# Moving the load of X's second slice from ScalarE's DMA queue to SP's, behind the first slice of G

## The chip, the core and the metric

The kernel runs on one core of one Trainium2 chip. The metric is the device time in microseconds (us) of one launch. Before the change it is 163.57 us, the median of three runs (163.35 to 163.69). The profiled execution has a span of 161.9 us from its first to its last instruction; all moments below are counted from the start of that span.

## What is computed

```python
def setup_inputs():
    batch, m, k, n = 16, 512, 1024, 768
    input:       float32 [16, 512, 1024]
    grad_output: float32 [16, 512, 768]

def reference(input, grad_output):
    return np.einsum('bmk,bmn->kn', input, grad_output)   # float32 [1024, 768]
```

It is one matrix product, X^T G, with X of 8192 x 1024 and G of 8192 x 768; the sum runs over all 8192 rows. The inputs are float32 in HBM; the kernel multiplies in bf16 and adds up in float32.

## The kernel before

**Tiling.** The 8192 rows are cut into 64 slices of 128 rows, one row to a partition. A slice is X of 128 x 1024 and G of 128 x 768. The output is cut into four quarters: A and B are the upper 512 rows (left and right 384 columns), C and D the lower 512 rows (left and right). A quarter has four strips of 128 rows; one strip of one quarter for one slice is one matmul, 128 x 128 weights of X against 128 x 384 of G, into one of the eight PSUM banks. So a slice taken plainly costs 16 matmuls, in four visits of four.

**Pairs.** The string `LOADS` (L12) says how the 32 pairs of slices are taken: "s" as two plain slices, "P" as one pair that is multiplied by a scheme with seven products of half-size blocks in place of eight. The sums of blocks that it needs are made by VectorE (DVE) ahead of time (L125 to L154), and its products m, n, o, p, q, A and D are added up in `macc` and `acc`. The first seven pairs (slices 0 to 13) and the last two are plain.

**Order.** The order of the work on TensorE (PE), VectorE, ScalarE (ACT) and GpSimd (POOL) is written out by hand: `manual_schedule` (L77) keeps each engine's instructions as the program gives them. `ORDER` (L16) is the list of visits. In "C2:4!0,0,0,0" the letter is the quarter or product, 2 the slice up to which it is carried, 4 how many of its strips ScalarE evicts from PSUM (VectorE does the others), and "!" that the banks are evicted after the visit. The first visits are A1 (slice 0, quarter A, four matmuls; its first strip is evicted by VectorE, the other three by ScalarE), D1 (slice 0, quarter D), C2 (slices 0 and 1, quarter C: eight matmuls, for each strip slice 0 and then slice 1), B2, D3, A2, B4 and so on. The first matmul on slice 1 is thus the second one of C2, the tenth of the real work.

**How the data come.** There are three ways in, all in front of the loop over `ORDER`:

- SP's queue loads G of slice 0 as float32 into `gf`, the left half at L81 and the right half at L83.
- ScalarE's queue loads X of slice 0 into `xf[0]` (L82) and, behind it, X of slice 1 into `xf[1]` (L84), both float32.
- POOL's queue loads everything else, G of slice 1 first (L111), then X and G of slices 2 and 3 (L113, L111), then whole pairs (L106, L107). These transfers turn float32 into bf16 on the way. They are issued in the order of use, as early as buffers come free; 14 pair buffers of each kind (`PAIRS_HELD`) stand for them, two of the X buffers being `xf`.

**Rounding.** What came as float32 is rounded to bf16 by `round_by` (L206), in pieces, partly on VectorE and partly on ScalarE. For slice 0: the left half of G and the whole of X ahead of the first visit (L209 to L215). The right half of G is rounded by VectorE between A1 and D1 (L360), so on VectorE it stands behind the eviction of A1's first strip (L301). X of slice 1 is rounded just ahead of C2:

```python
            round_by("DVE", x1, xf[1], 4 * P, 6 * P)
            round_by("ACT", x1, xf[1], 6 * P, 8 * P)
            round_by("DVE", x1, xf[1], 0, 2 * P)
            round_by("ACT", x1, xf[1], 2 * P, 4 * P)
```

C2 reads columns 4P to 8P of it, B2 the others. While the first transfers run, twelve matmuls on constants (L89) keep TensorE busy.

Of the kernel before, what the change touches and what calls it, by code (L numbers as in the profile page):

```python
# [9 lines left out]
P = 128  # L10
# [32 lines left out]
def kernel(  # L43
# [6 lines left out]
    nc = tc.nc  # L50
# [10 lines left out]
    X = input.rearrange("b m k -> (b m) k")  # L61
# [17 lines left out]
    xf = [pairs.tile([P, K], f32, name=f"xf{s}", tag="xp") for s in range(2)]  # L79
# [1 line left out]
    nc.sync.dma_start(out=gf[:, 0:NH], in_=G[0:P, 0:NH])  # L81
    nc.scalar.dma_start(out=xf[0], in_=X[0:P, :])  # L82
    nc.sync.dma_start(out=gf[:, NH:N], in_=G[0:P, NH:N])  # L83
    nc.scalar.dma_start(out=xf[1], in_=X[P : 2 * P, :])  # L84

    ones = nc.const_aps.tensor(1.0, (P, P), bf16)
    wps = psum.tile([P, 512], f32, name="bank7")
# [313 lines left out]
```

## Time and profile before

| what | value |
|---|---|
| time | 163.57 us (163.35 to 163.69) |
| span of the profiled execution | 161.9 us, granted clock 1.000 |
| TensorE busy | 157.1 us, 97% |
| VectorE, ScalarE, POOL busy | 139.6, 94.6, 34.6 us |
| read from HBM, written to it | 58.72 MB, 3.15 MB |
| first real matmul, end of A1 | 5.21 us, 6.17 us |
| start of D1 | 7.12 us |
| end of the last matmul | 158.42 us |

The page's first part gives busy time by engine, its second the span in 40 slices, and its fourth the chain of work that ended last. The rate of the DMA engines is counted by the bytes that they write. The transfers that turn float32 into bf16 write half of what they read, so that a stretch with only these shows half of the rate at which HBM is read. The timeline gives start, length, engine, line and tile of instructions, with the idle time ahead of them and what ended it in square brackets. For a transfer, the view of a tile gives the time from its issue to its landing.

### The profile page before, as it was taken

The page shows a single profiled execution, that of the slowest core. Times are in us where ns is not written, and L with a number is a line of the kernel's source. Part 1 is how long each engine was busy: PE and PEld are TensorE (multiplying, and loading weights), DVE is VectorE, ACT ScalarE, POOL GpSimd, SP SyncE. Part 2 cuts the span into 40 slices and gives each one's busy share as a digit, 9 for nine tenths or more (in the row PEclk, how much of TensorE's full clock was granted, in tenths as well). Part 3 has the DMA queues.
Part 4 walks back from the last instruction along what each step waited for, and adds up shares of the span by engine and source line. Part 5 has one row for each costly group of instructions (what it writes and reads, how often), then busy time and mean ns, then how long its engine had stood idle before and what let it go on. Part 6 is the DMA issues. An engine that isn't in the chain of part 4 may idle for free.

```text
span 161.9 us, 2755 instructions
## 1 busy us (share of the span) xinstructions
PE 157.1 (97%) x951; PEld 92.7 (57%) x951; DVE 139.6 (86%) x289; ACT 94.6 (58%) x221; POOL 34.6 (21%) x69
## 2 busy tenths in 40 slices
PE   8799999999999999999999999999999999999992
PEld 2365666566565565655656666666555666666661
DVE  0557947469979999999989999999998999999992
ACT  3766004745587799359749684661446646888410
POOL 7442222122221212222212222222212100000000
PEclk9999999999999999999999999999999999999999
DMA  5999999999999999999999999999999999902675
GB/s 171 294 213 211 211 216 215 211 211 215 214 213 212 212 213 213 213 211 215 212 213 213 212 216 214 220 207 212 211 211 214 212 214 214 187 5 97 225 283 173
DMA packets 12397, 33.40 MB, mean 206 GB/s; under 512 B 1376, under 2 KB 4192, under 8 KB 12384
## 3 DMA queue, kind: packets, MB, share of 16 engines
q0 software_dynamic: 9360, 28.64, 89.4%
q1 hardware_dynamic: 2592, 3.47, 6.2%
q10 hardware_dynamic: 432, 1.11, 1.8%
q8 instruction: 7, 0.11, 0.3%
q14 instruction: 6, 0.05, 0.1%
HBM read 58.72 MB, written 3.15 MB: 382 GB/s over the span
## 4 chain that ended last, share of the span: by engine, by line
PE 93%; DMA 3%; DVE 1%; SPq 0%; issue 0%
PE bank L285 93%; DMA gf<-in_grad_output_dram 3%; PE bank L336 0%; DVE acc L344 0%; SPq L81 0%; DVE gp L206 0%
## 5 line engine op out<-in xcount | busy, mean ns | idle before, releaser
L285 PEld LDWEIGHTS <-xp 128*128 128x128 bf16 x649 | 63.3, 98 | 43.6 <-issue 1.5
L285 PE MATMUL bank<-gp,xp 128*128 128x384 bf16 x468 | 80.9, 326 | 1.0 <-DVE gp L206 1.0
L299 ACT COPY macc<-bank 128x384 f32<-128x384 f32 x73 | 31.5, 493 | 25.0 <-PE bank L285 24.9
L303 DVE TENSOR_TENSOR acc<-bank,acc 128x384 f32<-128x384 f32 x69 | 34.7, 551 | 8.7 <-PE bank L285 8.3
L285 PEld LDWEIGHTS <-xe 128*128 128x128 bf16 x276 | 26.6, 98 | 18.5 <-DVE xe L145 0.8
L285 PE MATMUL bank<-ge,xp 128*128 128x384 bf16 x181 | 33.6, 326 | 0.0
L285 PE MATMUL bank<-gp,xe 128*128 128x384 bf16 x184 | 32.4, 326 | 0.0
L266 ACT COPY bank<-macc 128x384 f32<-128x384 f32 x56 | 25.3, 503 | 8.0 <-DVE macc L303 6.9
L299 ACT COPY acc<-bank 128x384 f32<-128x384 f32 x44 | 19.5, 486 | 15.4 <-PE bank L285 15.3
L107 POOL DMA_DIRECT2D xp<-in_input_dram x30 | 15.9, 530 | 53.1 <-DMA xp<-in_input_dram 29.8
L106 POOL DMA_DIRECT2D gp<-in_grad_output_dram x30 | 15.9, 531 | 37.5 <-DMA gp<-in_grad_output_dram 14.8
L303 DVE TENSOR_TENSOR macc<-bank,macc 128x384 f32<-128x384 f32 x44 | 22.5, 552 | 1.5 <-PE bank L285 1.2
L266 ACT COPY bank<-acc 128x384 f32<-128x384 f32 x34 | 15.2, 492 | 8.6 <-DVE acc L303 8.5
L285 PE MATMUL bank<-ge,xe 128*128 128x384 bf16 x92 | 16.6, 326 | 0.0
L145 DVE TENSOR_TENSOR xe<-xp 128x1024 bf16<-128x1024 bf16 x23 | 15.7, 684 | 0.5 <-DMA xp<-in_input_dram 0.5
L154 DVE TENSOR_TENSOR xp<-xp 128x1024 bf16<-128x1024 bf16 x23 | 15.7, 684 | 0.0
L189 DVE TENSOR_TENSOR acc<-acc,macc 128x768 f32<-128x768 f32 (+1 forms) x20 | 14.6, 791 | 0.0
L131 DVE TENSOR_TENSOR ge<-gp 128x768 bf16<-128x768 bf16 x23 | 12.7, 551 | 0.2 <-DMA gp<-in_grad_output_dram 0.2
L140 DVE TENSOR_TENSOR gp<-gp 128x768 bf16<-128x768 bf16 x23 | 12.7, 551 | 0.0
L149 DVE TENSOR_TENSOR xe<-xp 128x512 bf16<-128x512 bf16 x23 | 9.6, 418 | 0.0
L135 DVE TENSOR_TENSOR ge<-gp 128x384 bf16<-128x384 bf16 x23 | 8.1, 351 | 0.0
L89 PE MATMUL bank<-const-bfloat16-1.0 128*128 128x512 bf16 (+1 forms) x12 | 4.6, 574 | 0.8 <-PEq L385 0.8
(20 smaller groups left out, 21.4 us busy)
## 6 DMA issues: line engine op xcount, KB each, us to landing
xp<-in_input_dram POOLq DMA_DIRECT2D x30, 512.0 KB, 16.7
gp<-in_grad_output_dram POOLq DMA_DIRECT2D x30, 384.0 KB, 16.7
out_dram<-acc SPq DMA_DIRECT2D x15, 192.0 KB, 1.9
xf<-in_input_dram ACTq DMA_DIRECT2D x2, 512.0 KB, 5.0
gp<-in_grad_output_dram POOLq DMA_DIRECT2D x3, 192.0 KB, 6.6
xp<-in_input_dram POOLq DMA_DIRECT2D x2, 256.0 KB, 7.9
gf<-in_grad_output_dram SPq DMA_DIRECT2D x2, 192.0 KB, 4.6
out_dram<-acc SPq DMA_DIRECT2D x1, 128.0 KB, 1.7
```

Of the source, the lines that this page charges most:

```text
L106: nc.gpsimd.dma_start(out=gp, in_=G[rows, :].rearrange("(p m) n -> p m n", m=2))
L107: nc.gpsimd.dma_start(out=xp, in_=X[rows, :].rearrange("(p m) k -> p m k", m=2))
L131: nc.vector.tensor_add(out=ge[:, 0:2, :], in0=g[:, :, 0, :], in1=g[:, :, 1, :])
L140: nc.vector.tensor_sub(out=g[:, 1:3, :], in0=g[:, 1:3, :], in1=g[:, 3::-3, :])
L145: nc.vector.tensor_add(out=xe[:, 0:2, :].rearrange("p a k -> p (a k)"), in0=xp[:, 0, :], in1=xp[:, 1, :])
L149: nc.vector.tensor_add(out=extra[i][0][:, 2, :], in0=xp[:, 0, 0:KH], in1=xp[:, 1, KH:K])
L154: nc.vector.tensor_sub(out=x[:, 1:3, :], in0=x[:, 1:3, :], in1=x[:, 0::3, :])
L189: op(out=dst, in0=dst, in1=src)
L266: nc.scalar.copy(out=bank, in_=sum_of(p, q))
L285: nc.tensor.matmul(bank, stat, mov, start=opening and j == 0 and not carried, stop=close and j == len(items_now) - 1, skip_group_check=car ...
L299: nc.scalar.copy(out=dst, in_=bank)
L303: nc.vector.tensor_add(out=dst, in0=bank, in1=dst)
```

## The change

One line is different: the load of X of slice 1 is issued by SP rather than by ScalarE.

```diff
     nc.sync.dma_start(out=gf[:, 0:NH], in_=G[0:P, 0:NH])
     nc.scalar.dma_start(out=xf[0], in_=X[0:P, :])
     nc.sync.dma_start(out=gf[:, NH:N], in_=G[0:P, NH:N])
-    nc.scalar.dma_start(out=xf[1], in_=X[P : 2 * P, :])
+    nc.sync.dma_start(out=xf[1], in_=X[P : 2 * P, :])
```

Before, the right half of G of slice 0 (on SP's queue) and X of slice 1 (on ScalarE's) are under way at the same time. With the change they stand in one queue, G ahead of X, which is the order in which D1 and C2 use them. Nothing else differs: ScalarE has one instruction less, SP one more, ahead of the stores of the output that it issues at the end; the instructions of TensorE, VectorE and POOL stand as before.

## The prediction

> **What bounds the kernel now.** I read the page's chain of work that ended last first, then the same chain in order of time.
>
> ```profile
> PE 93%; DMA 3%; DVE 1%; SPq 0%; issue 0%
> ...
> 1.17 5.52 DMA gf<-in_grad_output_dram
> 6.69 0.02 issue
> 6.71 0.37 DVE gp L206
> 7.08 0.04 issue
> 7.12 150.51 PE bank L285 x921
> ```
>
> The end is set by one transfer, the right half of G of slice 0 (landed at 6.69), its rounding on VectorE, and then TensorE without a break to 157.6. So whatever moves D1's start at 7.12, or makes TensorE wait later, shows in the time. The waits of the first 16 us and the timeline of VectorE say how much is lost there:
>
> ```profile
> PE bank L285 <- DVE gp L206: 1.0, 1, 1.0
> ...
> 4.85 0.56 DVE L206 CAST xp<-xf 128x128 bf16<-128x128 f32 x3
> 5.72 0.56 DVE L301 COPY acc<-bank 128x384 f32<-128x384 f32 x1 [0.30 <-PE bank L285]
> 6.71 0.36 DVE L206 CAST gp<-gf 128x384 bf16<-128x384 f32 x1 [0.43 <-DMA gf<-in_grad_output_dram]
> 7.11 0.50 DVE L206 CAST xp<-xf 128x256 bf16<-128x256 f32 x2
> ```
>
> TensorE idles 0.96 us ahead of D1. VectorE is free for the rounding from 6.28 (5.72 + 0.56), so only 0.43 us of that can be won by an earlier landing. The last row is X of slice 1, landed at 1.17 + 5.9 = 7.07.
>
> Does a lead won at 7.12 last to the end? Weight loads are where TensorE's waits on data show. All their waits on a transfer, and where it is in their timeline:
>
> ```profile
> PEld L285 <- DMA xp<-in_input_dram: 0.3, 1, 0.3
> ...
> 43.93 0.44 PEld L285 LDWEIGHTS <-xp 128*128 128x128 bf16 x4 [0.28 <-DMA xp<-in_input_dram]
> ```
>
> This is X of the second "P" pair, issued at 26.02, landed 17.9 us later. Matmuls start 0.163 us apart; at this one the step is 0.226 us, a wait of 0.06 us. Up to 43.9 us the kernel is thus held by the stream of loads as well: TensorE arrives there 0.06 us early. A lead won at 7.12 ends in this wait, unless POOL's stream moves too; a lag over 0.06 us goes to the end whole.
>
> So I need the stream. Rates from the view by stretches (last column GB/s, by bytes written):
>
> ```profile
> 3.75:4.00 0.25, 0.25 (x2) 0.12 (x1) 0.00 (x0) 0.00 (x0) 0.25 (x2) 1.00 1.10 445
> 4.00:4.25 0.25, 0.25 (x2) 0.10 (x1) 0.00 (x0) 0.00 (x0) 0.25 (x2) 1.00 0.87 328
> ...
> 5.00:5.25 0.25, 0.25 (x4) 0.22 (x2) 0.25 (x3) 0.25 (x2) 0.25 (x2) 1.00 1.01 397
> 5.25:5.50 0.25, 0.25 (x3) 0.12 (x2) 0.17 (x1) 0.25 (x2) 0.25 (x1) 1.00 1.07 369
> 5.50:5.75 0.25, 0.25 (x3) 0.17 (x2) 0.03 (x1) 0.06 (x1) 0.10 (x1) 1.00 1.11 348
> 5.75:6.00 0.25, 0.25 (x3) 0.13 (x2) 0.25 (x1) 0.12 (x1) 0.00 (x0) 1.00 0.96 272
> ...
> 6.75:7.00 0.25, 0.00 (x0) 0.00 (x0) 0.25 (x1) 0.25 (x1) 0.00 (x0) 1.00 1.13 197
> ```
>
> The engines are busy throughout. A rate near 400 means float32 loads of SP and ScalarE; near 200 means POOL's, which write half of what they read. So POOL's loads, issued from 1.23 on, move nothing before about 5.3.
>
> The packet records of the trace (queue, start, duration and size of each packet) say why. A transfer of 128 rows is eight rows on each of 16 engines. A row of a half of G takes 65 ns, a row of X 159 ns, a row of POOL's G 134 ns, and an engine takes the queues with work in turn. Three facts matter:
> - SP's G ends on the 16 engines one by one, most from 5.17 to 5.63. The records don't name the engine, but for 11 of the 16 ends a row of POOL's starts 0.159 to 0.163 us later, which is one row of X, and POOL's first row is at 5.33. So POOL gets no turn on an engine while SP's and ScalarE's queues both have work there.
> - Between two transfers of one queue an engine pauses that queue for about 0.3 us (SP's left half ends at 3.71 to 4.14 on the engines, the right half begins 0.3 us later; ScalarE's at 4.03 to 4.46 likewise).
> - In ScalarE's pause SP has the engine alone, and so moves over half of the right half.
>
> **What the skill says.** The Trainium skill, "DMA: Bandwidth & Descriptors", section "Issuing engines are not separate DMA queues", says that transfers from all issuers share the same 16 engines and interleave, and that more issuers save only issue time. The trace agrees on the sharing (rates stay near 400 whoever moves). The same page, "Queues, rings and completion order", says that an engine goes round the queue rows it has work for. The trace shows this for SP with ScalarE and for ScalarE with POOL, but not for the three together. For the order within a queue I rely on the trace's records above.
>
> **The change part by part.**
> - ScalarE loses one issue (0.46 us at 1.17), SP gains one. ScalarE's next work waits for data until 4.52, and SP issues nothing else before the stores: zero.
> - X of slice 0 and the left half of G are untouched up to their ends at about 4.1. A1 stays at 5.21.
> - From 4.1 on ScalarE's queue is empty. The question is who takes its place. By the first fact above, POOL: one of the two queues that kept it out has drained. Then on an average engine the right half of G alternates with POOL: 8 x (65 + 134) = 1.6 us, against 0.3 us alone (4.6 rows) and 3.4 x (65 + 159) = 0.76, together 1.06, before. It lands 0.5 us later: 7.2 in place of 6.69; D1 starts at 7.6.
> - X of slice 1 then starts at 4.1 + 1.6 + 0.3 = 6.0 and needs 8 x (159 + 134) = 2.34 us, so ends at about 8.3. Before, it ended at 6.20 to 6.74, about 6.5, and landed at 7.07. So it lands 1.8 us later, at about 8.9.
> - Waiting behind it: on VectorE the piece for C2 (0.29 us), on ScalarE the piece for C2's last two strips (0.40 us), and behind TensorE's tenth matmul the whole rest. That matmul can start at 8.87 + 0.04 + 0.29 + 0.05 = 9.25. Before, it stood at 7.12 + 5 x 0.163 = 7.94. Lag: 1.3 us. The other pieces of X are done by 9.8 and needed from 9.9, so add nothing.
> - POOL's stream is no slower: what X of slice 1 gives up, POOL gets. G of slice 1 (before: landed at 1.23 + 6.3 = 7.53) comes over 1 us earlier, but isn't what C2 waits for.
> - The lag hides the 0.06 us wait at 43.9. Sum: +1.3 - 0.06 = +1.25, 164.8 us.
>
> For X's landing, which the trace doesn't show in this queue, the bounds are: alone on the engines from the start, 4.1 + 0.52 + 0.3 + 1.27 = 6.2 (landing about 6.8); sharing with POOL throughout, 8.3 (landing 8.9), half a us more if one slow engine lags as it does for the right half of G (most engines done by 5.6, the last at 6.34). I take 8.9: POOL's rows were waiting, and alternate one to one with ScalarE's as soon as SP is done.
>
> **The rivals.**
> - *SP goes ahead of POOL until its queue is empty.* The trace would look the same before, since it never shows POOL beside SP. Then the right half of G lands before 6.28, D1 starts at 6.28 + 0.36 + 0.04 = 6.7, X of slice 1 lands at 6.8, in time. But POOL begins at 6.2 on an average engine, where before it began at 5.45 and had done 0.5 us of work by 6.5, as if begun alone at 6.0; and in SP's pause of 0.3 us nothing moves. POOL's stream is 0.2 to 0.3 us late, and so is the load at 43.9, which eats the lead: 163.8 us. For it: POOL starts exactly when SP is done. Against it: there is no reason why SP should shut POOL out where ScalarE doesn't.
> - *Nothing to be measured.* X of slice 1 has a slack: landing at 7.07 + 0.04 + 0.29 + 0.05 = 7.45 against 7.94, so 0.5 us. If sharing costs no more than that and POOL's stream is unmoved, TensorE is at 43.9 as before: 163.5 us.
> - *Faster.* D1 starts at 6.7 (a lead of 0.43), and POOL's stream comes earlier by as much, for instance because one pause less is exposed (the rate falls to 328 in one quarter of a us at a change of transfers): 163.1 us. Against it: the engines are busy throughout before, so there is hardly idle DMA time to win, and the bytes ahead of the load at 43.9 are the same.
>
> **How the numbers follow.** POOL shares with SP: 0.62, 164.8 us. SP first: 0.22, 163.8. Nothing: 0.08, 163.5. Faster: 0.08, 163.1. The bound of 0.2% is 0.33 us. The first case is slower; the second, at +0.2 to +0.3, is mostly within and is counted as 0.04 slower and 0.18 same. So faster 0.08, same 0.26, slower 0.66. The range from 163.6 to 165.3 holds the first two cases with a late engine's 0.5 us above; it leaves out the other two.
>
> **What would show it.** If right: the rates fall below 350 from about 4.3 on rather than from 5.5; the right half of G lands near 7.2, X of slice 1 near 8.9, G of slice 1 over 1 us earlier than 7.53; TensorE waits ahead of C2 for the rounding of X (L206), ending near 9.25; no wait of the weight loads at 43.9. It is wrong if X lands before 7.6: then POOL was kept out (rates near 400 until 6), and a longer wait for a load by 44 us shows that rival. It would also be wrong if TensorE's lag were won back after 10 us, though no idle time is there to win it from.

## The result and the profile after

The changed kernel takes 164.38 us (164.29 to 164.44) against 163.63 us before in the same comparison: 0.75 us more, a ratio of 1.0049 with a 95% interval from 1.0031 to 1.0066. Here and below times are medians of all executions, ratios are estimated from the fast ones alone, and a part of the executions (14 of 156 of the kernel before, 8 of 22 of e7_left_by_pool below) takes about 1.5 us more than the rest, so that a ratio is not quite the quotient of the times beside it. The profiled execution after took 164.29 us, with a span of 162.5 us against 161.9.

The chain of work that ended last, in order of time, of the changed kernel (start, length, what; SPq is SP issuing a transfer):

```profile
1.17 0.42 SPq L83
1.60 0.05 issue
1.65 6.50 DMA xf<-in_input_dram
8.15 0.02 issue
8.18 0.31 DVE xp L206
8.48 0.05 issue
8.53 149.68 PE bank L285 x916
...
159.01 0.68 DVE acc L344 x2
```

Another transfer now stands at its head. Before, it was the right half of G, landed at 6.69, with 921 matmuls behind it. Now it is X of slice 1, landed at 8.15, with 916 behind it, so the last wait has moved from D1's first matmul to the tenth, C2's first on slice 1. Before, that one started at 7.12 + 5 x 0.163 = 7.93; it now starts 0.60 us later. The last VectorE piece of the chain starts 0.57 us later than before, where it was this line:

```profile
158.44 0.68 DVE acc L344 x2
```

The timeline of TensorE shows both sides of the change:

```profile
6.42 0.97 PE L285 MATMUL bank<-gp,xp 128*128 128x384 bf16 x5 [0.43 <-DVE gp L206]
8.53 21.69 PE L285 MATMUL bank<-gp,xp 128*128 128x384 bf16 x132 [1.13 <-DVE xp L206]
```

D1 starts at 6.42 in place of 7.12, 0.70 us earlier. Not all of that is the change's doing. A1's matmuls ran at a faster pace in this execution (the first step is 0.172 us rather than 0.307), so that VectorE began to evict its first strip at 5.55 rather than 5.72. By this estimate the earlier landing itself is worth 0.70 - 0.17, about 0.5 us; the prediction's 0.43 was a little low, since the rounding starts 0.47 us after the eviction, not 0.56. Five matmuls later TensorE stops for 1.13 us, for the rounding of X. The timeline of VectorE names the cause, a transfer:

```profile
6.02 0.35 DVE L206 CAST gp<-gf 128x384 bf16<-128x384 f32 x1
8.18 0.50 DVE L206 CAST xp<-xf 128x256 bf16<-128x256 f32 x2 [1.80 <-DMA xf<-in_input_dram]
```

G's right half no longer holds its rounding back: it landed 4.1 us after its issue at 1.17, at 5.27, or 1.4 us earlier than before. X of slice 1 lands 6.50 us after its issue at 1.65. The rates by stretches (last column, GB/s by bytes written; POOL's loads write half of what they read) show what moved in between:

```profile
4.50:4.75 0.25, 0.25 (x2) 0.15 (x1) 0.22 (x1) 0.25 (x1) 0.25 (x2) 1.00 1.17 289
4.75:5.00 0.25, 0.25 (x3) 0.00 (x1) 0.21 (x2) 0.25 (x2) 0.25 (x2) 1.00 1.22 219
5.00:5.25 0.25, 0.25 (x4) 0.18 (x3) 0.25 (x3) 0.25 (x2) 0.25 (x2) 1.00 1.13 223
5.25:5.50 0.25, 0.25 (x3) 0.18 (x3) 0.13 (x1) 0.25 (x1) 0.25 (x1) 1.00 1.08 256
5.50:5.75 0.25, 0.25 (x4) 0.17 (x2) 0.20 (x1) 0.04 (x1) 0.09 (x1) 1.00 0.99 328
5.75:6.00 0.25, 0.25 (x2) 0.02 (x1) 0.25 (x1) 0.25 (x1) 0.00 (x0) 1.00 1.12 377
```

The engines are busy, but from 4.75 to 5.25 the rate (219 and 223) is near that of POOL's loads alone. Then it rises again towards that of float32 loads: X of slice 1 is well under way only from about 5.5. So POOL did not share with G, as I had forecast; it went between G and X.

### The profile page after: what moved, and what is told of

Same layout as the page of the kernel before. It is cut to its first block, busy times and chain, and to the rows that moved or that the text cites. A ratio compares the mean times of both kernels' runs of the same rounds, so it can differ in the third digit from the quotient of the medians.

```text
span 162.5 us, 2755 instructions
## 1 busy us (share of the span) xinstructions
PE 157.0 (97%) x951; PEld 92.5 (57%) x951; DVE 139.3 (86%) x289; ACT 94.5 (58%) x221; POOL 34.6 (21%) x69
## 4 chain that ended last, share of the span: by engine, by line
PE 93%; DMA 4%; DVE 1%; SPq 0%; issue 0%
PE bank L285 92%; DMA xf<-in_input_dram 4%; PE bank L336 0%; DVE acc L344 0%; SPq L83 0%; SPq L81 0%; DVE xp L206 0%
```

## Experiments

All comparisons are against the kernel before, run beside it on the same chip. The packet records of the trace have queue, start, duration and size of each packet. For the kernels that bear on the order of the transfers they give this table (moments in us). A transfer's rows end on an engine with a packet of 4 bytes; "median" is over these on the 16 engines, while a transfer lands only when the last engine is through. "16 rows started" is when sixteen rows had begun, about one on each engine; landings are from the view of the tile. In e8, "POOL's" and X are smaller loads, see below.

```
kernel           place of X     G's right half   POOL's      X of slice 1:    rows end,  landed
                 in its queue   ends, median     first row   16 rows started  median
before           second         5.43             5.33        4.59             6.53       7.1
changed          third          4.61             4.48        5.57             7.46       8.15
e1_swap          second         6.42             5.31        4.12             6.04       6.8
e2_mirror        third          4.52             4.42        5.57             7.34       8.63
e3_pool_waits    third          4.70             4.51        5.61             7.01       8.04
e6_pool_late     third          4.72             6.85        4.85             6.01       6.55
e8 (half of X)   third          4.68             4.45        5.27             6.10       6.7
e11_g_whole      second         4.57 (all of G)  5.33        4.79             6.44       7.2
```

**The two hardware queues exchanged**, in the kernel before and in the changed one. This asks whether SP's queue as such keeps POOL out.

```diff
 e1_swap, against the kernel before
-    nc.sync.dma_start(out=gf[:, 0:NH], in_=G[0:P, 0:NH])
-    nc.scalar.dma_start(out=xf[0], in_=X[0:P, :])
-    nc.sync.dma_start(out=gf[:, NH:N], in_=G[0:P, NH:N])
-    nc.scalar.dma_start(out=xf[1], in_=X[P : 2 * P, :])
+    nc.scalar.dma_start(out=gf[:, 0:NH], in_=G[0:P, 0:NH])
+    nc.sync.dma_start(out=xf[0], in_=X[0:P, :])
+    nc.scalar.dma_start(out=gf[:, NH:N], in_=G[0:P, NH:N])
+    nc.sync.dma_start(out=xf[1], in_=X[P : 2 * P, :])
 e2_mirror: the same, but the last line stays on G's queue
+    nc.scalar.dma_start(out=xf[1], in_=X[P : 2 * P, :])
```

> The kernel before with the two hardware queues exchanged: G of slice 0 in two halves on ScalarE's queue, X of slices 0 and 1 on SP's. Both traces so far have POOL's first row on an engine at the end of the right half of G there, whether ScalarE's queue still holds X (before, 5.2 to 5.6) or is empty (after, 4.5 to 4.9). Theory 1, SP's queue keeps POOL out until it pauses or drains: POOL's first rows now come at SP's change from X of slice 0 to X of slice 1 (4.0 to 4.4) or only when SP is done (above 6.2), not at the end of G. With POOL in from 4.2 on, three queues share, the right half of G lands after 7 and the time is 164 or more. Theory 2, it is the third hardware transfer on an engine that has to end, on whatever queue: POOL's first rows at 5.2 to 5.6, the right half of G lands near 6.7, time as before, 163.4 to 163.8.

> The changed kernel with the two hardware queues exchanged: ScalarE's queue has both halves of G and behind them X of slice 1, SP's has X of slice 0 alone. Theory 1 (SP's queue keeps POOL out): SP is empty from 4.0 to 4.4, so POOL starts there, shares the engines with the right half of G, which lands at about 6.2, and X of slice 1 lands near 8.9; D1 at 6.6 to 6.8, C2's first matmul on slice 1 near 9.2, time near 164.9. Theory 2 (the third hardware transfer on an engine has to end): all as in the changed kernel, POOL from 4.5 to 4.9, the right half of G at 5.3, X of slice 1 at 8.15, time 164.4.

Measured: e1_swap 164.10 against 163.48 us, ratio 1.0040 (1.0005 to 1.0076); e2_mirror 164.96, ratio 1.0071 (1.0049 to 1.0094). Both theories fail on e1_swap. The first had the time and G's late landing (7.20), but POOL's first row is not at SP's change of transfers near 4.1. The second had the moment of that row (5.31), but not what it waits for, since G's end comes only after 6, nor the time. In that trace all three queues move rows on the engines at once, so there is no rule that POOL waits for a queue to be done. In e2_mirror, POOL starts at 4.42, X at 5.57, all much as in the changed kernel, whichever engine issues them; X lands later still, at 8.63, since one engine was late (its last packet at 8.13, the median at 7.34).

These two kernels also give the price of a lag. From their chains, e1_swap first:

```profile
7.63 150.49 PE bank L285 x921
...
158.93 0.68 DVE acc L344 x2
```

```profile
9.01 149.69 PE bank L285 x916
...
159.50 0.68 DVE acc L344 x2
```

In e1_swap D1 starts 0.51 us later than before, and the last VectorE piece 0.49 us later. In e2_mirror C2's first matmul on slice 1 starts 1.08 us later, and the last piece 1.06 us later. A lag goes to the end one for one here.

**What POOL's transfers cost X of slice 1.** In e3_pool_waits POOL issues one load and then waits for X; in e6_pool_late it issues none before the right half of G has landed.

```diff
 e3_pool_waits, against the changed kernel, behind the load of G of slice 1 (L111)
+                if s == 1:
+                    late = accp.tile([P, 1], f32, name="late")
+                    nc.gpsimd.tensor_copy(out=late, in_=xf[1][:, 0:1])
 e6_pool_late, against the changed kernel, ahead of POOL's first load
+    late = accp.tile([P, 1], f32, name="late")
+    nc.gpsimd.tensor_copy(out=late, in_=gf[:, NH : NH + 1])
```

> The changed kernel, but POOL issues G of slice 1 alone and then waits for X of slice 1 (a copy of one column) before it issues the rest. It measures what POOL's stream costs X of slice 1. Sharing with POOL is the cause of the late landing: X of slice 1 lands at 6.9 to 7.3 in place of 8.15, and C2's first matmul on slice 1 starts at 7.4 to 7.7. If the late landing comes from SP's queue itself (a long pause between its transfers, as the 0.85 us seen between the right half of G and X of slice 1): it lands at 7.6 or later. POOL's stream starts late here, by up to 1 us, so the time is no measure: TensorE will wait for slices 2 to 5 instead, 163.8 to 164.8.

> The changed kernel, but POOL waits for the right half of G of slice 0 (a copy of one column) before it issues its first load. In the changed kernel X of slice 1 starts 0.85 us after the end of the right half of G on an engine, and G of slice 1 from POOL's queue moves in between; with only that one load in POOL's queue X still landed at 8.04. Theory, POOL's first load fills the pause and pushes X back: without it X starts 0.3 us after G's end, at 4.9 to 5.1, runs alone and ends at 6.2 to 6.4 on most engines; it lands at 6.6 to 7.0. Rival, SP's pause ahead of its third transfer is long by itself: X starts at 5.4 or later and lands at 7.3 or later. POOL's whole stream starts about 2 us late, so TensorE waits for slices 1 to 5 and the time, 165 to 168, tells nothing.

Measured: X lands at 1.65 + 6.39 = 8.04 in e3_pool_waits. So the stream behind POOL's first load costs the landing only 0.1 us; the median engine, though, was through 0.45 us earlier (7.01 in place of 7.46). By what I expected, that spoke for SP's queue as the cause; the next kernel says otherwise. X lands at 6.55 in e6_pool_late, 1.6 us earlier. The view of the tile xf of e6_pool_late gives issue to landing of its two loads, of which the longer is that of slice 1:

```profile
DMA to landing us min/median/max: 4.1/4.5/4.9
```

Its rates by stretches:

```profile
4.50:4.75 0.25, 0.25 (x3) 0.10 (x1) 0.22 (x1) 0.22 (x1) 0.00 (x0) 1.00 1.30 387
4.75:5.00 0.25, 0.07 (x2) 0.00 (x0) 0.19 (x3) 0.25 (x2) 0.00 (x0) 1.00 0.91 361
5.00:5.25 0.25, 0.11 (x1) 0.10 (x1) 0.25 (x3) 0.25 (x2) 0.00 (x0) 1.00 1.11 459
```

It is issued at 1.65. The hollow is gone; float32 rates go on without a break. So it is POOL's first load, G of slice 1, that goes ahead of X and costs it about 0.7 us at the start (16 rows started by 5.57 with it, by 4.85 without); SP's queue does not pause for long by itself. The rest of the 1.6 us is lost after the start, 0.45 us of it, on the median engine, to the stream behind that load (e3 against the changed kernel). In e8 below, where POOL's first load is half as large, sixteen rows of X had started by 5.27. The times of e3 and e6 (168.08 and 166.24 us, one execution each) are no measure, since POOL's stream starts late there and TensorE waits for it.

**The lag taken away, the transfers kept.** This kernel leaves out X of slice 1 in quarters C and D, so its result is not the product: the pieces that C2 needs are rounded from X of slice 0, which is there.

```diff
 e5_no_x1_wait, against the changed kernel
-            round_by("DVE", x1, xf[1], 4 * P, 6 * P)
-            round_by("ACT", x1, xf[1], 6 * P, 8 * P)
+            round_by("DVE", x1, xf[0], 4 * P, 6 * P)
+            round_by("ACT", x1, xf[0], 6 * P, 8 * P)
```

> The changed kernel with the two pieces that C2 needs of slice 1 rounded from X of slice 0 in place of X of slice 1 (so slice 1 enters quarters C and D with wrong X); all transfers are as in the changed kernel. TensorE then keeps its lead from D1 (6.42 against 7.12 before) until G of slice 1 lands at about 7.5: C2's first matmul on slice 1 at 7.6, 0.35 us ahead of the kernel before. As predicted, the wait at 43.9 us for X of the second P pair ends any lead: 163.5 us, and a wait of weight loads for a transfer is seen before 44 us. Rival: that load was late in that one trace only, the stream has slack, and the lead stays to the end: 163.1 to 163.3 us.

Measured: 163.93 against 163.48 us, ratio 1.0021 (1.0004 to 1.0037). Against the changed kernel's ratio of 1.0049, about half of the loss is gone, though the two intervals overlap a little. The profiled execution, 163.68 us with a span of 161.9, is the second fastest of the twenty, so the loss that is left isn't traced. The kernel does not test the lead as meant. The other two pieces of slice 1 still wait for the transfer, and on ScalarE one of them stands ahead of C2's evictions, as its timeline shows:

```profile
8.06 0.40 ACT L206 CAST xp<-xf 128x256 bf16<-128x256 f32 x1 [0.43 <-DMA xf<-in_input_dram]
8.38 1.61 ACT L299 COPY acc<-bank 128x384 f32<-128x384 f32 x4
```

B2 takes over C2's banks, so TensorE, 0.47 us ahead at C2's first matmul on slice 1 (7.46), waited there, until 8.90, and for each strip after it; by 15.3 us it stood where the kernel before does. A late transfer reaches more than the matmul that needs it: it holds what is queued behind the rounding.

**Can the lead be kept without the lag?** Four kernels take X of slice 1 out of third place, in whole or in part.

```diff
 e7_left_by_pool, against the changed kernel (the roundings of columns 0 to 4P fall away)
-    nc.sync.dma_start(out=xf[1], in_=X[P : 2 * P, :])
+    nc.sync.dma_start(out=xf[1][:, KH:K], in_=X[P : 2 * P, KH:K])
 and behind the load of G of slice 1
+                if s == 1:
+                    nc.gpsimd.dma_start(out=xp[:, h, 0:KH], in_=X[P : 2 * P, 0:KH])
 e8_left_g_halves: the same, with G of slice 1 in two loads
+                if s == 1:
+                    nc.gpsimd.dma_start(out=gp[:, h, 0:NH], in_=G[P : 2 * P, 0:NH])
+                    nc.gpsimd.dma_start(out=xp[:, h, 0:KH], in_=X[P : 2 * P, 0:KH])
+                    nc.gpsimd.dma_start(out=gp[:, h, NH:N], in_=G[P : 2 * P, NH:N])
 e9_x1_by_pool, against the changed kernel (all four roundings of slice 1 fall away)
-    nc.sync.dma_start(out=xf[1], in_=X[P : 2 * P, :])
 and ahead of all other loads of POOL
+            if s == 1:
+                nc.gpsimd.dma_start(out=xp[:, h, :], in_=X[s * P : (s + 1) * P, :])
 e10_x1_by_pool_d4: the same, and in ORDER
-D5 D6!0,0,0,0
+D4 D6!0,0,0,0
```

> The changed kernel with X of slice 1 divided: SP loads only the right half that C2 needs (behind G), POOL loads the left half that B2 needs as bf16, behind G of slice 1; its two roundings fall away. If the lag comes from the landing of X of slice 1 alone, the right half lands at 6.9 to 7.3, C2's first matmul on slice 1 starts at 7.5 to 7.7 (G of slice 1 lands at 7.0 to 7.5), and TensorE is 0.2 to 0.4 us ahead of the kernel before. If the lead stays to the end: 163.1 to 163.4. If it ends in the wait for a load at 43.9 us, as I predicted for a lead: 163.5. If the left half comes late (over 8.6), TensorE waits ahead of B2 and it is 163.5 to 164.

> As the last one, and POOL loads G of slice 1 in two halves, left half, then the left half of X of slice 1, then the right half of G, so that C2's matmuls on slice 1 need less from POOL. If G of slice 1 is what ends last ahead of C2 once X comes in time, its first matmul on slice 1 starts 0.1 to 0.3 us earlier than in the last kernel, at 7.2 to 7.5. Two more issues on POOL (0.5 us each) and more, smaller transfers can put POOL's stream 0.1 to 0.3 us back: 163.0 to 163.5 where the lead stays, 163.5 to 163.8 where the stream binds.

> X of slice 1 is loaded by neither hardware queue but by POOL, as bf16 and ahead of everything else that it loads, so its four roundings fall away. The first part of the change, the right half of G alone behind X of slice 0, is kept without the second, X behind it. G's right half lands at 5.2 to 5.4, D1 starts at 6.3 to 6.5, X of slice 1 lands at 6.3 to 6.8 and G of slice 1 at 7.2 to 7.6: C2's first matmul on slice 1 at 7.3 to 7.7, a lead of 0.2 to 0.6 us over the kernel before. Theory, the lead ends in the stream of loads: TensorE waits at about 16.5 us for X of slice 4, and the time is that of before, 163.4 to 163.8. Rival, the stream leaves room: 163.0 to 163.3.

> As the last one, with the visits D5 D6 turned into D4 D6: the four matmuls on slice 3 come ahead of the first on slice 4, which is thus needed three matmuls, 0.49 us, later. If the wait for X of slice 4 is what ate the lead, it falls away, and the lead reaches the next load (X of slice 6, first used 0.2 us after its landing in the kernel before): 0.1 to 0.3 us faster than the last kernel, 163.2 to 163.5. If nothing changes, the stream as a whole binds: the waits only move to X of slices 6 and 8 or to 44 us.

| kernel | time, before beside it | ratio (95%) | D1 starts | C2's first matmul on slice 1 (before: 7.93) |
|---|---|---|---|---|
| e7_left_by_pool | 164.19, 163.61 | 1.0045 (1.0019 to 1.0072) | 6.65 | 8.11 |
| e8_left_g_halves | 164.08, 163.61 | 1.0032 (1.0006 to 1.0058) | 6.44 | 7.25 |
| e9_x1_by_pool | 164.07, 163.52 | 1.0030 (1.0017 to 1.0043) | 6.65 | 7.88 |
| e10_x1_by_pool_d4 | 164.14, 163.52 | 1.0026 (1.0008 to 1.0044) | 6.48 | 7.99 |

None is faster than before, and each is slower than I had put it at most. e8 is the telling one: TensorE runs from D1 through C2 without a wait, 0.68 us ahead of the kernel before, and its time is longer all the same. The timeline of its weight loads (PEld) from 9 to 17 us:

```profile
10.09 1.74 PEld L290 LDWEIGHTS <-xp 128*128 128x128 bf16 x12 [0.47 <-DMA xp<-in_input_dram]
12.25 3.75 PEld L290 LDWEIGHTS <-xp 128*128 128x128 bf16 x24 [0.42 <-DMA xp<-in_input_dram]
16.60 0.44 PEld L290 LDWEIGHTS <-xp 128*128 128x128 bf16 x4 [0.60 <-DMA xp<-in_input_dram]
```

Three times it waits for a load of X by POOL, of slices 2, 3 and 4, and at the third TensorE starts at 16.61 us, later than the 16.45 at which the kernel before gets there without waiting. In e9 the same wait ends at 16.57, in e7 at 16.93. e10 moves the first use of slice 4 back by three matmuls; the wait at 16.6 goes, and the weight loads wait for X of slice 6 instead (0.36 us, to 21.03) and again at 44.29. In e7 the right half of X came later than I had put it, and in e9 and e10 G of slice 1 did, so that there was little or no lead at all at C2.

So a lead runs into POOL's stream, load by load. But these kernels lost more than a lead: X of slice 4 landed at 16.50 to 16.92 in the four, against 16.29 before. In the changed kernel, too, it landed at 16.58 (TensorE, itself late, did not wait for it), but in e5, with the same loads, at 16.19. Why the stream comes later in some traces than in others is not settled. At the end the traces of e7 to e10 are 0.61, 0.13, 0.31 and 0.38 us behind; the median of e8 is 0.47 us behind, so most of its loss is not traced.

One more thing ties the stream together. It is not issued just as buffers come free, as I had written. POOL's ninth load comes only when an earlier load has landed; from the timeline of POOL in e9:

```profile
6.81 0.53 POOL L105 DMA_DIRECT2D gp<-in_grad_output_dram  x1 [1.21 <-DMA xp<-in_input_dram]
```

X of slice 1, its first load there, had landed at 6.54. In the kernel before the ninth is issued at 7.83, after G of slice 1 landed at 7.53; in e8 at 6.06, after a landing at 5.77.

**A control, and G in one transfer.**

```diff
 e12_before_d4, against the kernel before, in ORDER
-D5 D6!0,0,0,0
+D4 D6!0,0,0,0
 e11_g_whole and e13_g_whole_timed, against the changed kernel
-    nc.sync.dma_start(out=gf[:, 0:NH], in_=G[0:P, 0:NH])
+    nc.sync.dma_start(out=gf, in_=G[0:P, :])
     nc.scalar.dma_start(out=xf[0], in_=X[0:P, :])
-    nc.sync.dma_start(out=gf[:, NH:N], in_=G[0:P, NH:N])
     nc.sync.dma_start(out=xf[1], in_=X[P : 2 * P, :])
```

> The kernel before with D4 D6 in place of D5 D6, as a control. TensorE doesn't wait for X of slice 4 there (lands at 16.3, first matmul at 16.4), so the time is that of before within 0.1%: 163.4 to 163.8. If it is faster by 0.1 us or more, a small wait ahead of slice 4 was hidden in the pipelined matmuls.

> The changed kernel with G of slice 0 in one transfer, so that X of slice 1 is the second transfer of SP's queue and not the third. Theory, POOL's waiting first load (G of slice 1) takes the engines when SP's queue changes from G to X, and X follows when that load is through: X starts about 0.8 us after G's end and lands at 7.9 to 8.3. Rival, the long pause belongs to the third transfer of a queue: X starts 0.1 to 0.3 us after G's end (near 4.8) and lands at 6.6 to 7.3. A1 starts later here, at 5.4 to 5.7, since it waits for the whole of G; time 163.9 to 164.5 in the first case, 163.5 to 163.8 in the second.

> The kernel with G of slice 0 in one transfer again, now timed in rounds. X of slice 1 stands behind G on SP's queue as in the changed kernel, but in second place. Theory, what costs time is the third place in the queue, where POOL's first load gets in ahead of X, and a lead is of no use because of the stream of loads: X lands at 7.0 to 7.4, D1 starts near 6.9, and the time is that of the kernel before within 0.1%, 163.4 to 163.7. Rival, X behind G on one queue is slower in itself and the single time of 163.56 was a lucky one: 164.0 or more.

Measured: e12_before_d4 163.54 against 163.52 us, ratio 1.0010 (0.9981 to 1.0040). By chance its trace shows what the change was after, with the loads as they were: the right half of G landed at 1.17 + 4.8 = 5.97 rather than 6.69, so the same landing differs by 0.7 us between two executions with the same loads; D1 started at 6.43. C2's first matmul on slice 1 came 0.44 us ahead of the trace of before. The waits of its weight loads, from their timeline:

```profile
20.52 0.11 PEld L285 LDWEIGHTS <-xp 128*128 128x128 bf16 x2 [0.36 <-DMA xp<-in_input_dram]
...
43.66 0.28 PEld L285 LDWEIGHTS <-xp 128*128 128x128 bf16 x3 [0.31 <-DMA xp<-in_input_dram]
```

At these two the steps between matmuls are 0.301 and 0.251 us in place of 0.163, so 0.14 and 0.09 us of the lead go, and 0.28 us are left in the span of that execution (the kernel before loses 0.06 at its own wait at 43.9). The tenth matmul waited for G of slice 1, landed at 7.45: a lead of D1 beyond 0.44 us would have ended there already.

e11_g_whole took 163.56 us in one execution; e13_g_whole_timed, the same kernel in thirteen, 163.71 against 163.62 us, ratio 0.9998 (0.9981 to 1.0015). It keeps X behind G on SP's queue, in second place, and loses nothing; nor does it win a lead, since A1 now waits for the whole of G (D1 starts at 6.95 and 7.10). X starts about 0.2 us after G's end and lands at 7.2, and POOL's first row is at 5.33. So my theory for it, that POOL gets in whenever SP's queue changes from G to X, is refuted. SP's queue as such did not cost the time, but X's third place in it, with all that goes with that place.

**What stays open.** In every trace in which X was the second transfer of its queue, it started ahead of POOL's first load; in every one in which it was third, behind it, unless POOL had issued nothing yet. Second place here also means issued at 1.17, just ahead of POOL's first issue at 1.23, and third place issued at 1.65, behind it. Service in order of issue would explain this as well as a limit of two transfers in a queue; no run tells them apart. Nor is it settled why POOL's first row comes near 5.3 in the one group and near 4.45 in the other. In the second group, and in e9 and e10, it starts 6 ns after the right half of G has ended on a first engine (4.473 and 4.479 in the changed kernel). In the first, nothing of the kind is seen: in e1_swap it starts while both other queues have rows to move.

## Why the prediction was right in sign and too large in size

- **X of slice 1 becomes the last wait, ahead of the tenth matmul, and its lag goes to the end whole:** right, and shown by the changed kernel, e1 and e2 (0.60, 0.51 and 1.08 us of lag; 0.57, 0.49 and 1.06 us at the end). e5 takes much of it away again.
- **"The question is who takes its place. By the first fact above, POOL":** this step failed. Once ScalarE's queue was empty, G's right half had the engines to itself and was through at 4.61 (median), not at 5.7. It landed at 5.27, not 7.2, and D1 started at 6.42, held by VectorE's eviction and rounding, not at 7.6. I had drawn a rule from one trace, that POOL gets no turn while both hardware queues have work. e1_swap refutes it, and it says nothing on the case with one queue empty.
- **X's landing, forecast 8.9, was 8.15.** This is the term of the sum that was mis-sized. X began one POOL load after G (16 rows started by 5.57 instead of 6.0), and its rows ended at 7.46 (median) rather than 8.3. With 8.15 in place of 8.87, the same sum as in the prediction gives 8.53 for the tenth matmul, as measured, and a lag of 0.60 in place of 1.3 us. That the start of X was not further off is in part luck: two errors went against each other. G's right half ended 1.1 us earlier than forecast, and the pause between it and X, put at 0.3 us, was 0.96 us, because POOL's first load went in between.
- **The rival with SP ahead of POOL** was half right: SP did go first for G, but not for X, which POOL's first load overtook. Its landing of 6.8 is what e6 shows without POOL (6.55).
- **"A lead won at 7.12 ends in this wait" at 43.9:** right that leads run into the stream of loads (e8, e12), wrong that one load is the wall. Leads were eaten at X of slices 2, 3 and 4 (e8), at slice 6 and at 43.7 (e12). The load of X at 43.9 is not fixed either: in the changed kernel it landed at 25.91 + 17.0 = 42.9, issued and landed by the same view as before.
- **"POOL's stream is no slower", and G of slice 1 "over 1 us earlier":** wrong. G of slice 1 landed at 7.5 as before, though POOL began 0.85 us sooner; one engine was late with it (its last packet after 7.2, most by 6.4). X of slices 2, 3 and 4 landed 0.3 to 0.4 us later than before in that trace; TensorE, later by 0.60, did not wait for them.
- **"rates stay near 400 whoever moves"** holds only if POOL's loads are counted by what they read: the 197 that the prediction shows, counted by bytes written, is then 394.
- **Signs that I named:** no wait of weight loads at 43.9, right; rates under 350, from 4.5 rather than 4.3, but only to 5.75, and from POOL's load alone rather than from a sharing with G; X late and TensorE waiting for its rounding, right.

The measured times differ by 0.75 us, the profiled spans by 0.6. The profiled execution of the changed kernel was the shortest of its four (164.29 against a median of 164.38), and that of the kernel before, 163.70, lay above its median of 163.63, so the 0.60 us traced is a little less than what the medians show.

## What to carry to other kernels

When a load is moved in a queue, write down not only what it is taken away from but what it now stands behind, in every queue that shares the engines: here the transfer that was helped landed 1.4 us earlier, of which its user, D1, could take about 0.5, and the one put third landed 1.1 us later. A gain at the start of a kernel such as this one is worth at most the slack of the loads that come next; look at the first use of each of them against its landing before going after it. And a rule on how queues share, drawn from one arrangement, is a guess for another until the two queues have been exchanged.

## What the runs showed of the hardware that was not expected

- POOL's loads, issued from 1.23 us on, moved their first row only at 4.3 to 5.3 us in the traces above (where POOL did not have to wait), 3 to 4 us after the issue. In e6, where POOL began to issue at about 5.5, it took 1.3 us (first row at 6.85).
- A transfer in third place on SP's queue, issued 0.42 us after POOL's first load, was overtaken by that load nearly whole: 108 of its 128 rows had started when 16 of X had. These 16 had started by 5.57 with it, by 4.85 without, and by 5.27 when it was half as large.
- The first four real matmuls do not always run at full pace: in e5, e7 and e9 they are 0.320 us apart; in the kernel before only the first step is so long (0.307 us), in the changed kernel none, with a granted clock of 1.0 in the profile at these moments. A1's last matmul starts at 6.17 in e5 and at 5.67 in the changed kernel for this reason, and D1 at 6.65 and 6.42. What decides it, no run shows.
